# A two-block network in fp32: weight splits of 1024 columns on ScalarE and VectorE in three buffers, in place of 512 columns with GpSimd in six

## The chip, the cores and the metric

One Trainium2 chip, one core. The metric is the device time of one execution in microseconds; lower is better. The kernel before was run three times: median 714.41 us, 713.59 to 714.75.

## What is computed

Two transformer-like blocks, in fp32, on 256 tokens of width 1024.

```python
"block 1"
z = rms_norm(x) @ w_in
q, c_kv, q_idx, k_idx, w_idx, g_attn, x_rnn, g_rnn, merge = split_cols(z)
o = sparse_mla_attention(q, rms_norm(c_kv), q_idx, layer_norm(k_idx), w_idx, w_uk, w_uv)  # top 64 keys by an index score
y_attn = (o * silu(g_attn)) @ w_attn_proj
h = rg_lru(causal_depthwise_conv(x_rnn), ...)             # gates, then a scan over the tokens
y_rnn = (h * silu(g_rnn)) @ w_rnn_proj
x = x + (sigmoid(merge_a) * y_attn + sigmoid(merge_r) * y_rnn) @ w_out
"block 2"
c_q, c_kv, k_r, q_b, k_b, v_b, gate_a, gate_b = jnp.split(rmsnorm(x) @ w_in_2, ...)
o_a = mla_attention(c_q, c_kv, k_r, w_uq, w_ukv)          # low-rank queries, keys, values; rope
o_b = moba_attention(q_b, k_b, v_b)
x = x + (sigmoid(gate_a) * (o_a @ w_o_mla) + sigmoid(gate_b) * (o_b @ w_o_moba)) @ w_out_2
x = x + hierarchical_moe(rmsnorm(x))                      # 32 experts, two of them per token
```

## The kernel before

All weights lie in one array in DRAM, cut into pieces of 1 MB (128 partitions x 2048 fp32), in the order of use. A ring of slots in SBUF takes them (21 of `bigp`, more once the dense part is over); activations that live long take slots of the same ring. SP issues the loads in the order of the pieces, each as soon as its slot is free.

The **dense part** multiplies with fp32 accuracy from three fp32r products. `split` (L233 to L246) takes 512 columns of a piece: ScalarE rounds them to fp32r (`h`, L244), and the rest `l = w - h` is taken by VectorE or GpSimd in turn (L245, `POOLDIV = 2`). `mm3` (L248) then issues h x h and h x l for each k (L254) and l x h (L257). The results of `split` lie in six buffers of 4 KB a partition (`hlp` four, `hl2` two, one split in three). The activations' own high and low halves are made once (`xh`, `xl`; `split_out`, L362 and L363).

`dense_fm` (L263) makes a feature-major result of 256 columns from a piece in four splits of 12 matmuls each; `dense_tm` (L289) makes a token-major one. `dense_tm_last` is the last product before the experts. The names of the pieces tell the stage, in the order of the program: `A`, `qi`, `xr` (input of the recurrence), `q`, `mr`, `ma` (merge gates), `gr`, `rp`, `ga`, `ap`, `wo` (block 1), `cq`, `uq`, `ukv`, `qb`, `kb`, `vb`, `g2a`, `oa`, `g2b`, `ob`, `w` (block 2), then the experts (`gu`, `dn`).

Between the dense pieces, `tick` emits small work from a list: the picks of the top keys (`pick`, L520; the eighth makes the mask `dm`, L527 to L530), the heads' keys and values from `ukuv` (`head_k`, L532, four of 256 columns; `head_v`, two of 512), the recurrence's convolution (`rnn_conv`, L590), gates (`rnn_gate`, L597) and scans (`rnn_scan`, L616; GpSimd's product L620, VectorE's scan L621), and the attention (`ps_s`, L376, the scores; L383, mask and maximum; L384, exponential; L385 and L387, division; `pt`, L394, transposes; `po`, the values). A gate is: `pg` on TensorE (L603), two `rt` on ScalarE (L606), `la` and `tt` (L608, L609), and three VectorE instructions (L611 to L613). `xc`, `rt`, `tt`, `xr`, `wk`, `g` and others are tiles of one pool of seven, `s2p` (NS2 = 7).

In block 2, `p_uq` (three accumulators of 256 columns by two token halves, `mm`, three buffers for all dense products) is evacuated to `qtm` (L878, ScalarE), `p_ukv` to `ktm` and `vm` (L889, L890); the rope on `qtm` is VectorE's (L825 to L828), and `ptm` (L910) transposes them.

The order on each engine is made by the framework's scheduler from the order of the program, estimated durations and priorities. A split, and most evacuations, are emitted `with tc.high_priority(offset=AHEAD)`, AHEAD = 150, which lets them pass what was emitted shortly before. Each engine then runs its own list in order and waits by semaphores.

The **experts** need 64 pieces `gu` and 32 pieces `dn`, multiplied in plain fp32 (L1233, L1260).

Of the kernel before, what the change touches and what calls it, by code (L numbers as in the profile page):

```python
# [17 lines left out]
P = 128  # L18
T = 256
# [5 lines left out]
FILL = -2e38  # L25
NBIG, NMO, NS2, SPARE, POOLDIV = 21, 4, 7, 0, 2
KW = 5
# [52 lines left out]
def tile_two_blocks(ctx: ExitStack, tc: tile.TileContext, w, xT_d, xtk_d, vecs_d, rows_d, consa_d, consb_d, wr_d, lam_d, out_d):  # L80
    nc = tc.nc
# [5 lines left out]
    hl_stack, right_stack = ExitStack(), ExitStack()  # L87
    hlp = [hl_stack.enter_context(tc.tile_pool(name="hlp", bufs=4)), right_stack.enter_context(tc.tile_pool(name="hl2", bufs=2, side="right"))]
    dn = right_stack.enter_context(tc.tile_pool(name="dn", bufs=1, side="right"))
# [142 lines left out]

    def split(view, nk, width, eng=None, small=False):  # L233

        n = nk * width
        if small:
            h, l = (s2(x, F32R)[:, :n].rearrange("p (k c) -> p k c", k=nk) for x in ("h", "l"))
        else:
            hl = (hlp[1] if len(hlp) > 1 and nsplit[0] % 3 == 0 else hlp[0]).tile([P, 1024], F32R, tag="hl", name="hl")
            h, l = (hl[:, o:o + n].rearrange("p (k c) -> p k c", k=nk) for o in (0, 512))  # L240
        nsplit[0] += 1
        e = eng or (nc.gpsimd if nsplit[0] % POOLDIV == 0 else nc.vector)
        with tc.high_priority(offset=AHEAD):
            nc.scalar.activation(h, view, AF.Copy)  # L244
            e.tensor_tensor(l, view, h.bitcast(F32), ALU.subtract)  # L245
        return h, l  # L246
# [16 lines left out]
    def dense_fm(ps, name, rh, rl, nk=8, width=T, c0=0, late=False):  # L263


        wv = piece(name)[:, :nk * width].rearrange("p (k c) -> p k c", k=nk)

        def part(j, q):
            c = c0 + j * P
            h, l = split(wv[:, 4 * q:4 * q + 4, c:c + P], 4, P)  # L270
            return ps[:, j * T:(j + 1) * T], (lambda k: h[:, k - 4 * q, :]), (lambda k: l[:, k - 4 * q, :]), rh, rl
        if late:

            for j in range(2):
                mm3(*part(j, 0), range(4), j == 0, False)
            tick()
            parts = [part(j, 1) for j in range(2)]
            for ks in ((4, 5), (6, 7)):
                for j in range(2):
                    mm3(*parts[j], ks, False, j == 1 and ks[0] == 6)  # L280
        else:
            nq = nk // 4
            for j in range(2):
                for q in range(nq):
                    mm3(*part(j, q), range(4 * q, 4 * q + 4), q == 0, q == nq - 1)
                if j == 0:
                    tick()

    def dense_tm(pss, name, ah, al, nk=8, width=T):  # L289

        wv = piece(name)[:, :nk * width].rearrange("p (k c) -> p k c", k=nk)
        n = min(512 // width, nk)
        one = pss[0] is pss[1]
        for q in range(0, nk, n):
            h, l = split(wv[:, q:q + n, :], n, width)
            for b in range(2):

                mm3(pss[b][:, (b * T if one else 0):][:, :width],
                    lambda k: ah[:, k, b * P:(b + 1) * P], lambda k: al[:, k, b * P:(b + 1) * P],
                    lambda k: h[:, k - q, :], lambda k: l[:, k - q, :], range(q, q + n),  # L300
                    q == 0 and (b == 0 or not one), q + n == nk and (b == 1 or not one))
            if q + n == nk // 2:
                tick()

    def dense_tm_last(pss, name, ah, al, split_done, done):
# [226 lines left out]
    def head_k(i):  # L532
# [999 lines left out]
```

## Time and profile before

| | |
|---|---|
| median of 3 runs | 714.41 us (713.59 to 714.75) |
| the profiled execution | 713.6 us |
| its span, first to last instruction | 711.6 us |
| mean granted clock of TensorE | 0.983 |
| VectorE busy | 416.7 us, 59% of the span, 1035 instructions |
| ScalarE busy | 324.7 us, 46%, 714 instructions |
| GpSimd busy | 238.6 us, 34%, 194 instructions |

The busy time of an engine is a sum over the span, so it hides stages with other limits; the tables by stretches show them. Starts are in microseconds from the span's first instruction. A line such as `L245 DVE TENSOR_TENSOR hl<-w_xr,hl` is one of `split` for the piece `xr`; PE is TensorE, DVE is VectorE, ACT is ScalarE, POOL is GpSimd. Where several instructions are merged into one row (x3), the time runs from the first one's start to the last one's end; consecutive instructions of an engine overlap a little in the records, so the step from one start to the next is what each takes of its engine's time.

### The profile page before, as it was taken

How to read it: one execution, taken by the hardware profiler on the slowest of the kernel's cores; microseconds unless marked ns; L12 is line 12 of the kernel's file. 1: busy time of each engine (PE TensorE's matmuls, PEld its weight loads, DVE VectorE, ACT ScalarE, POOL GpSimd, SP SyncE). 2: the span in 40 equal slices, each digit the busy share in tenths (PEclk: the TensorE clock that was granted, in tenths of full speed). 3: DMA queues.
4: the chain of work that ended last, by engine and by line, in shares of the span. 5: the costliest groups of instructions: out<-in, count | busy, mean ns of one | idle time of the engine just before them, and what ended most of it. 6: DMA issues, size and time to landing. Idle time of an engine off the chain costs nothing. (4 is left out here: it accounts for less than half of the span.)

```text
span 711.6 us, 13956 instructions
## 1 busy us (share of the span) xinstructions
PE 674.1 (95%) x5463; PEld 558.7 (79%) x5463; DVE 416.7 (59%) x1035; ACT 324.7 (46%) x714; POOL 238.6 (34%) x194
## 2 busy tenths in 40 slices
PE   7989999999999999999999999999999999989973
PEld 7989889789999999998999988999645445534532
DVE  4877998789555777889655574375532222222224
ACT  5455598765765656666466466555100000001022
POOL 1454344645535647864332322382000000000002
PEclk8999999999999999999999999999999999999997
DMA  8995116234557457451036615578899999999992
GB/s 314 416 421 212 55 30 252 84 125 172 181 195 275 157 167 292 174 177 66 5 132 221 227 70 195 221 302 319 326 414 421 419 420 420 420 420 420 420 408 76
DMA packets 26855, 178.69 MB, mean 251 GB/s; under 512 B 3104, under 2 KB 4000, under 8 KB 6176
## 3 DMA queue, kind: packets, MB, share of 16 engines
q1 hardware_dynamic: 26352, 177.15, 63.9%
q8 instruction: 45, 0.74, 0.4%
q10 hardware_dynamic: 432, 0.59, 0.2%
q14 instruction: 26, 0.21, 0.1%
HBM read 176.67 MB, written 1.05 MB: 250 GB/s over the span
## 5 line engine op out<-in xcount | busy, mean ns | idle before, releaser
L1316 POOL TENSOR_TENSOR xg<-xo,fin 128x256 f32<-128x256 f32 (+1 forms) x10 | 6.0, 632 | 206.6 <-DVE xo L1306 206.6
L1233 PE MATMUL pgu<-w_gu,xe 128*32 128x512 f32 x512 | 64.9, 597 | 0.4 <-DMA w_gu<-in_w_dram 0.4
L1238 ACT ACTIVATE th<-pgu,ss 128x256 f32<-128x256 f32 x8 | 3.8, 474 | 132.3 <-PE pgu L1233 132.3
L1263 DVE COPY ys<-py 128x256 f32<-128x256 f32 (+1 forms) x33 | 13.7, 416 | 41.8 <-PE py L1260 41.8
L1233 PEld LDWEIGHTS pgu<-w_gu,xe 128*32 128x32 f32 x512 | 14.8, 109 | 28.3 <-issue 25.2
L1197 PEld LDWEIGHTS px<-G,xT 128*128 128x128 f32 x256 | 30.2, 192 | 7.6 <-issue 5.5
L1199 DVE TENSOR_TENSOR xe<-px,vecs 128x256 f32<-128x256 f32 (+1 forms) x34 | 13.8, 409 | 37.3 <-PE px L1197 37.3
L384 ACT ACTIVATE lg<-lg,mx 128x128 f32<-128x128 f32 x64 | 28.3, 444 | 12.1 <-DVE mx L383 12.0
L1197 PE MATMUL px<-G,xT 128*128 128x128 f32 x256 | 31.9, 278 | 1.4 <-DVE G L1185 0.9
L254 PE MATMUL p_qkv<-hl,hh 128*128 128x256 f32 x192 | 33.0, 293 | 0.0
L1339 PE MATMUL acc<-ys,gwT 128*128 128x256 f32 x112 | 29.8, 398 | 2.9 <-DVE ys L1263 2.9
L1339 PEld LDWEIGHTS acc<-ys,gwT 128*128 128x128 f32 x112 | 19.5, 189 | 13.5 <-DVE ys L1263 6.0
L254 PEld LDWEIGHTS p_qkv<-hl,hh 128*128 128x128 f32 x192 | 27.5, 196 | 0.3 <-issue 0.2
L1239 DVE SCALAR_TENSOR_TENSOR th<-th,pgu 128x256 f32<-128x256 f32 x8 | 3.4, 422 | 37.1 <-ACT th L1238 37.1
L387 DVE TENSOR_SCALAR lg<-lg,sm 128x128 f32<-128x128 f32 x64 | 22.2, 391 | 0.8
L257 PE MATMUL p_qkv<-hl,hl__3328 128*128 128x256 f32 x96 | 20.0, 289 | 0.0
L595 DVE SCALAR_TENSOR_TENSOR xc<-xr,vecs,xc 128x256 f32<-128x256 f32 x24 | 18.1, 754 | 1.1 <-ACT xc L593 0.9
L245 POOL TENSOR_TENSOR hl<-w_g2a,hl 128x512 fp32r<-128x512 f32 x8 | 10.4, 1303 | 22.0 <-ACT hl L244 22.0
L254 PE MATMUL p_gr<-xh,hl 128*128 128x256 f32 x64 | 17.3, 299 | 0.0
L254 PE MATMUL p_gr<-xl,hl 128*128 128x256 f32 x64 | 17.3, 297 | 0.0
L245 POOL TENSOR_TENSOR hl<-w_rp,hl 128x512 fp32r<-128x512 f32 x8 | 11.9, 1496 | 15.5 <-ACT hl L244 15.5
L254 PE MATMUL p_cq<-hl__3328,hl 128*128 128x256 f32 x64 | 16.3, 285 | 0.6 <-DVE hl__3328 L755 0.6
(549 smaller groups left out, 2295.1 us busy)
## 6 DMA issues: line engine op xcount, KB each, us to landing
w_gu<-in_w_dram SPq DMA_DIRECT2D x64, 1024.0 KB, 18.2
w_dn<-in_w_dram SPq DMA_DIRECT2D x31, 1024.0 KB, 19.9
w_xr<-in_w_dram SPq DMA_DIRECT2D x4, 1024.0 KB, 11.3
w_q<-in_w_dram SPq DMA_DIRECT2D x4, 1024.0 KB, 17.2
w_mr<-in_w_dram SPq DMA_DIRECT2D x4, 1024.0 KB, 19.8
w_ma<-in_w_dram SPq DMA_DIRECT2D x4, 1024.0 KB, 12.4
w_gr<-in_w_dram SPq DMA_DIRECT2D x4, 1024.0 KB, 5.1
w_rp<-in_w_dram SPq DMA_DIRECT2D x4, 1024.0 KB, 4.9
```

The lines of the kernel that those rows point to most:

```text
L245: e.tensor_tensor(l, view, h.bitcast(F32), ALU.subtract)
L254: nc.tensor.matmul(out, l_(k), r_(k), start=first and i == 0, stop=last and i == n - 1)
L257: nc.tensor.matmul(out, al(k), bh(k), start=first and i == 0, stop=last and i == n - 1)
L384: nc.scalar.activation(lg[:, c0:c1], lg[:, c0:c1], AF.Exp, bias=mx[:, b:b + 1], scale=-1.0, accum_out=sm[:, b:b + 1])
L387: nc.vector.tensor_scalar(lg[:, c0:c1], lg[:, c0:c1], sm[:, b:b + 1], None, ALU.mult)
L595: nc.vector.scalar_tensor_tensor(xc[:, :T], xr[:, kk:kk + T], vec(V_CW, kk * 8 + m), xc[:, :T], ALU.mult, ALU.add)
L1197: nc.tensor.matmul(px[:, j * P:(j + 1) * P], x2[:, k, b, :], G[:, b], start=b == 0, stop=b == 1)
L1199: nc.vector.tensor_tensor(xg[k // 4][:, k % 4:k % 4 + n, :], v3(px, n, P), gain2(k, n), ALU.mult)
L1233: nc.tensor.matmul(pgu[32 * j:32 * j + 32, :], xg[k // 4][:, k % 4, 32 * j:32 * j + 32], wgu[:, 512 * j:512 * j + 512], start=k == 0, stop ...
L1263: nc.vector.tensor_copy(ys[:, :n], py[:, :n])
L1316: nc.gpsimd.tensor_tensor(xg[:, b, sl], xo[:, b, sl], fin[:, sl], ALU.mult)
L1339: nc.tensor.matmul(acc[0][:, b, c // 512, c % 512:c % 512 + n], lhsT, rhs, start=q == 0 and c % 512 == 0, stop=q == 6 and c % 512 == T)
```

## The change

Every split is done by ScalarE (`h`) and VectorE (`l`). A split takes 1024 columns in place of 512; there are three buffers of 8 KB in place of six of 4 KB. Pieces of 2048 columns have two splits; `dense_fm` emits both before its products, `dense_tm` takes 1024 columns at a time with its products in pairs of k (a piece of `uq`, 1536 columns, has a split of 1024 and one of 512, each with a buffer). `head_k`, `head_v`, `A` and the last split of `dense_tm_last` put their halves into two tiles of `s2p` and no longer count for the turn of the buffers. Priorities stay as they were.

```diff
-NBIG, NMO, NS2, SPARE, POOLDIV = 21, 4, 7, 0, 2
+NBIG, NMO, NS2, SPARE = 21, 4, 7, 0
...
-    hlp = [hl_stack.enter_context(tc.tile_pool(name="hlp", bufs=4)), right_stack.enter_context(tc.tile_pool(name="hl2", bufs=2, side="right"))]
+    hlp = [hl_stack.enter_context(tc.tile_pool(name="hlp", bufs=2)), right_stack.enter_context(tc.tile_pool(name="hl2", bufs=1, side="right"))]
...
-    def split(view, nk, width, eng=None, small=False):
+    def split(view, nk, width, small=False):
         n = nk * width
         if small:
             h, l = (s2(x, F32R)[:, :n].rearrange("p (k c) -> p k c", k=nk) for x in ("h", "l"))
         else:
-            hl = (hlp[1] if len(hlp) > 1 and nsplit[0] % 3 == 0 else hlp[0]).tile([P, 1024], F32R, tag="hl", name="hl")
-            h, l = (hl[:, o:o + n].rearrange("p (k c) -> p k c", k=nk) for o in (0, 512))
-        nsplit[0] += 1
-        e = eng or (nc.gpsimd if nsplit[0] % POOLDIV == 0 else nc.vector)
+            hl = (hlp[1] if len(hlp) > 1 and nsplit[0] % 3 == 0 else hlp[0]).tile([P, 2048], F32R, tag="hl", name="hl")
+            h, l = (hl[:, o:o + n].rearrange("p (k c) -> p k c", k=nk) for o in (0, 1024))
+            nsplit[0] += 1
         with tc.high_priority(offset=AHEAD):
             nc.scalar.activation(h, view, AF.Copy)
-            e.tensor_tensor(l, view, h.bitcast(F32), ALU.subtract)
+            nc.vector.tensor_tensor(l, view, h.bitcast(F32), ALU.subtract)
         return h, l
...
         wv = piece(name)[:, :nk * width].rearrange("p (k c) -> p k c", k=nk)
-
-        def part(j, q):
-            c = c0 + j * P
-            h, l = split(wv[:, 4 * q:4 * q + 4, c:c + P], 4, P)
-            return ps[:, j * T:(j + 1) * T], (lambda k: h[:, k - 4 * q, :]), (lambda k: l[:, k - 4 * q, :]), rh, rl
+        if nk == 8:
+            both = [split(wv[:, :, c0 + j * P:c0 + (j + 1) * P], 8, P) for j in range(2)]
+        else:
+            h2, l2 = split(wv[:, :, c0:c0 + 2 * P], nk, 2 * P)
+            both = [(h2[:, :, j * P:(j + 1) * P], l2[:, :, j * P:(j + 1) * P]) for j in range(2)]
+
+        def part(j, ks, first, last):
+            h, l = both[j]
+            mm3(ps[:, j * T:(j + 1) * T], lambda k: h[:, k, :], lambda k: l[:, k, :], rh, rl, ks, first, last)
...
-            nq = nk // 4
             for j in range(2):
-                for q in range(nq):
-                    mm3(*part(j, q), range(4 * q, 4 * q + 4), q == 0, q == nq - 1)
+                for k in range(0, nk, 4):
+                    part(j, range(k, k + 4), k == 0, k + 4 == nk)
                 if j == 0:
                     tick()
 
     def dense_tm(pss, name, ah, al, nk=8, width=T):
...
-        n = min(512 // width, nk)
         one = pss[0] is pss[1]
+        n = 1024 // width
         for q in range(0, nk, n):
-            h, l = split(wv[:, q:q + n, :], n, width)
-            for b in range(2):
...
+            m = min(n, nk - q)
+            h, l = split(wv[:, q:q + m, :], m, width)
+            for q2 in range(q, q + m, 2):
+                for b in range(2):
...
-            if q + n == nk // 2:
+            if q == 0:
                 tick()
 
     def dense_tm_last(pss, name, ah, al, split_done, done):
...
-        for q in (0, 2, 4, 6):
-            hls[q] = split(wv[:, q:q + 2, :], 2, T, nc.vector, small=q == 6)
+        h4, l4 = split(wv[:, 0:4, :], 4, T)
+        hls[0], hls[2] = ((h4[:, q:q + 2, :], l4[:, q:q + 2, :]) for q in (0, 2))
+        hls[4] = split(wv[:, 4:6, :], 2, T)
+        hls[6] = split(wv[:, 6:8, :], 2, T, small=True)
...
-        h, l = split(wA[:, 2 * q:2 * q + 2, :], 2, 200, nc.vector)
+        h, l = split(wA[:, 2 * q:2 * q + 2, :], 2, 200, small=True)
...
-        h, l = split(uu[:, i * T:(i + 1) * T].unsqueeze(1), 1, T)
+        h, l = split(uu[:, i * T:(i + 1) * T].unsqueeze(1), 1, T, small=True)
...
-        h, l = split(uu[:, 1024 + 512 * i:1536 + 512 * i].unsqueeze(1), 1, 512)
+        h, l = split(uu[:, 1024 + 512 * i:1536 + 512 * i].unsqueeze(1), 1, 512, small=True)
...
-        hl2 = [split(wv[:, k:k + 1, 512 * i:512 * i + 512], 1, 512) for k in range(2)]
+        h, l = split(wv[:, :, 512 * i:512 * i + 512], 2, 512)
...
```

The scheduler's lists change with it. Three places follow; names without numbers are tiles, and what an instruction waits for stands in brackets, by engine or DMA queue.

TensorE among the merge gates `p_mr`, where the heads' keys (`p_uk`) and the recurrence's gates (`pg`) are interleaved; before:

```order
476 L254 MATMUL p_mr<-xh,hl 128x256
477 L254 MATMUL p_mr<-xl,hl 128x256
478 L603 MATMUL pg<-xc,w_rg 64x256 [waits DVE_49,PE_49]
479 L603 MATMUL pg<-xc,w_rg 64x256 x3
480 L254 MATMUL p_mr<-xh,hl 128x256 [waits Activation_49]
```

and now:

```order
564 L253 MATMUL p_uk<-cT,h 128x256 [waits PE_49,Activation_49]
565 L253 MATMUL p_uk<-cT,h 128x256
566 L608 MATMUL pg<-xc,w_rg 64x256 [waits DVE_49]
567 L608 MATMUL pg<-xc,w_rg 64x256 x3
568 L256 MATMUL p_uk<-cT,l 128x256 [waits DVE_49]
569 L253 MATMUL p_uk<-cT,h 128x256 x2
570 L256 MATMUL p_uk<-cT,l 128x256
571 L253 MATMUL p_uk<-cT,h 128x256 [waits PE_49,Activation_49]
572 L253 MATMUL p_uk<-cT,h 128x256
573 L608 MATMUL pg<-xc,w_rg 64x256 [waits DVE_49]
574 L608 MATMUL pg<-xc,w_rg 64x256 x3
575 L256 MATMUL p_uk<-cT,l 128x256 [waits DVE_49]
```

Gates 2 to 5 and three `p_uk` stand in a row, with no `p_mr` between them.

ScalarE from the last splits of `uq` on, where `qtm<-p_uq` is the evacuation that frees an accumulator of `p_uq`; before:

```order
380 L244 ACTIVATE hl<-w_ukv 128x512 [waits DMAHW6_49,PE_49,Pool_49]
381 L244 ACTIVATE hl<-w_ukv 128x512 [waits PE_49,Activation_49]
382 L878 ACTIVATE qtm<-p_uq,sqk 128x256 [waits DVE_49]
383 L878 ACTIVATE qtm<-p_uq,sqk 128x256
384 L878 ACTIVATE qtm<-p_uq,sqk 128x256 [waits PE_49]
385 L878 ACTIVATE qtm<-p_uq,sqk 128x256
386 L244 ACTIVATE hl<-w_ukv 128x512 [waits Pool_49]
387 L244 ACTIVATE hl<-w_ukv 128x512 [waits PE_49,Activation_49]
388 L244 ACTIVATE hl<-w_qb_3331 128x512 [waits DMAHW7_49,PE_49,Pool_49]
389 L878 ACTIVATE qtm<-p_uq,sqk 128x256 [waits PE_49]
390 L878 ACTIVATE qtm<-p_uq,sqk 128x256
391 L244 ACTIVATE hl<-w_qb_3331 128x512 [waits Activation_49]
```

and now:

```order
298 L243 ACTIVATE hl<-w_uq_3010 128x1024 [waits DMAHW5_49,PE_49,Activation_49]
299 L243 ACTIVATE hl<-w_uq_3010 128x512 [waits PE_49,Activation_49]
300 L243 ACTIVATE hl<-w_ukv 128x1024 [waits DMAHW6_49,DVE_49,PE_49]
301 L243 ACTIVATE hl<-w_ukv 128x1024 [waits DVE_49,PE_49]
302 L243 ACTIVATE hl<-w_qb_3137 128x1024 [waits DMAHW7_49,DVE_49,PE_49]
303 L883 ACTIVATE qtm<-p_uq,sqk 128x256 [waits DVE_49]
304 L883 ACTIVATE qtm<-p_uq,sqk 128x256 x5
305 L894 ACTIVATE ktm<-p_ukv,sqk 128x4x64 [waits DVE_49,PE_49]
306 L895 ACTIVATE vm<-p_ukv,sqk 128x256
```

All evacuations of `p_uq` moved behind the splits of `ukv` and the first of `qb`.

VectorE at the start of the first attention (`ix<-la,yy` is the scan; `sm` and `lg<-lg,sm` the division; `lg,mx<-ps_s,dm` mask and maximum); before:

```order
217 L621 SCALAR_TENSOR_TENSOR ix<-la,yy 128x256 [waits Pool_49] x3
218 L245 TENSOR_TENSOR hl<-w_gr_855,hl 128x512 [waits Activation_49]
219 L385 RECIPROCAL sm<-sm 128x2 [waits Activation_49]
220 L383 ISA lg,mx<-ps_s,dm 128x128 [waits DVE_49,PE_49]
221 L383 ISA mx 128x1
222 L383 ISA lg,mx<-ps_s,dm 128x256
223 L383 ISA mx 128x1
224 L621 SCALAR_TENSOR_TENSOR ix<-la,yy 128x256 [waits Pool_49]
225 L387 TENSOR_SCALAR lg<-lg,sm 128x128 [waits DVE_49]
226 L387 TENSOR_SCALAR lg<-lg,sm 128x256
```

and now:

```order
226 L390 RECIPROCAL sm<-sm 128x2 [waits Activation_49]
227 L392 TENSOR_SCALAR lg<-lg,sm 128x128 [waits DVE_49]
228 L392 TENSOR_SCALAR lg<-lg,sm 128x256
229 L392 TENSOR_SCALAR lg<-lg,sm 128x128 [waits DVE_49]
230 L392 TENSOR_SCALAR lg<-lg,sm 128x256
231 L388 ISA lg,mx<-ps_s,dm 128x128 [waits DVE_49,PE_49]
232 L388 ISA mx 128x1
233 L686 TENSOR_TENSOR g<-p_ma,s_bc 128x512
234 L388 ISA lg,mx<-ps_s,dm 128x256
235 L388 ISA mx 128x1
236 L626 SCALAR_TENSOR_TENSOR ix<-la,yy 128x256 [waits Pool_49]
```

The divisions of the first heads stand ahead of all scans.

## Rows read from the trace of the kernel before

**Rows 1.** The page's busy time of each engine, share of the span, instructions.
```profile
PE 674.1 (95%) x5463; PEld 558.7 (79%) x5463; DVE 416.7 (59%) x1035; ACT 324.7 (46%) x714; POOL 238.6 (34%) x194
```

**Rows 2.** Stretches: us, busy (x instructions) by engine, PEclk, DMA share, GB/s.
```profile
240.00:260.00 20.00, 20.00 (x170) 20.00 (x170) 14.07 (x19) 12.01 (x21) 12.14 (x9) 1.00 0.49 171
540.00:560.00 20.00, 20.00 (x167) 10.70 (x163) 5.12 (x17) 0.47 (x1) 0.00 (x0) 1.00 1.01 421
```

**Rows 3.** TensorE's waits to 509 us: for whom, us in total, times, longest.
```profile
PE ptm L910 <- DVE qtm L828: 2.5, 1, 2.5
PE ps_s L376 <- DVE mx L383: 1.6, 1, 1.6
PE pt L394 <- DVE lg L387: 1.4, 2, 1.2
PE p_cq L254 <- DVE hl__3328 L755: 0.6, 2, 0.5
```

**Rows 4.** The same table of stretches, right behind two of these waits.
```profile
145.40:148.80 3.40, 3.40 (x17) 3.34 (x16) 3.40 (x8) 2.07 (x5) 1.09 (x1) 0.51 0.20 29
339.90:343.30 3.40, 3.40 (x19) 3.36 (x17) 2.37 (x4) 0.00 (x0) 0.00 (x0) 0.50 0.00 0
```

**Rows 5.** Instructions in time, VectorE and GpSimd, 335 to 339: start, us, what.
```profile
335.58 1.52 DVE L827 TENSOR_TENSOR qtm<-qtm,consb 128x256 f32<-128x256 f32 x1
337.62 1.49 DVE L827 TENSOR_TENSOR qtm<-qtm,consb 128x256 f32<-128x256 f32 x1
...
335.48 1.34 POOL L245 TENSOR_TENSOR hl<-w_qb,hl 128x512 fp32r<-128x512 f32 x1
337.56 1.27 POOL L245 TENSOR_TENSOR hl<-w_qb,hl 128x512 fp32r<-128x512 f32 x1 [0.74 <-ACT hl L244]
```

**Rows 6.** The same, 132 to 144, VectorE and GpSimd.
```profile
132.79 3.37 DVE L621 TENSOR_TENSOR_SCAN ix<-la,yy 128x256 f32<-128x256 f32 x3 [1.59 <-POOL yy L620]
139.83 3.30 DVE L621 TENSOR_TENSOR_SCAN ix<-la,yy 128x256 f32<-128x256 f32 x2
...
132.02 7.66 POOL L620 TENSOR_TENSOR yy<-yy,ix 128x256 f32<-128x256 f32 x8 [4.62 <-ACT yy L619]
139.64 4.56 POOL L245 TENSOR_TENSOR hl<-w_gr,hl 128x512 fp32r<-128x512 f32 x3
```

**Rows 7.** L245 to 509 us; groups (busy us, mean ns); one convolution step.
```profile
0.00:509.00 509.00, 122.01 (x144) 189.84 (x135) 0.99 0.53 199
...
L245 DVE TENSOR_TENSOR hl<-w_g2b,hl 128x512 fp32r<-128x512 f32 x8 | 5.5, 693 | 8.4 <-ACT hl L244 8.4
L363 DVE TENSOR_TENSOR oa<-po,oa 128x256 fp32r<-128x256 f32 x4 | 1.7, 425 | 3.1 <-ACT oa L362 3.1
L452 ACT ACTIVATE xtk<-xtk 128x1024 f32<-128x1024 f32 x2 | 2.1, 1048 | 1.4 <-DMA xtk<-in_xtk_dram 1.4
...
96.96 0.48 DVE L595 SCALAR_TENSOR_TENSOR xc<-xr,vecs,xc 128x256 f32<-128x256 f32 x1
```

**Rows 8.** ScalarE in time around one gate.
```profile
98.66 0.83 ACT L606 ACTIVATE rt<-pg,hb 128x256 f32<-128x256 f32 x2
99.37 0.60 ACT L608 ACTIVATE la<-rt,nsp 128x256 f32<-128x256 f32 x1
100.35 0.63 ACT L244 ACTIVATE hl<-w_mr 128x512 fp32r<-128x512 f32 x1
```

**Rows 9.** ScalarE's evacuations of p_uq, and first p_ukv on TensorE.
```profile
326.50 1.57 ACT L878 ACTIVATE qtm<-p_uq,sqk 128x256 f32<-128x256 f32 x4 [0.25 <-DVE sqk L862]
...
331.28 1.09 PE L254 MATMUL p_ukv<-hl,cqp 128*128 128x512 f32 x4
```

**Rows 10.** 80 to 120 us: all engines as in rows 2; then L595 alone.
```profile
80.00:120.00 40.00, 39.98 (x311) 35.29 (x310) 38.02 (x75) 33.35 (x71) 17.67 (x14) 1.00 0.37 131
...
80.00:120.00 40.00, 13.17 (x18) 1.00 0.37 131
```

More of the change, by code (lines that the diff above doesn't have):

```diff
@@ L266, in dense_fm @@
         wv = piece(name)[:, :nk * width].rearrange("p (k c) -> p k c", k=nk)
-        def part(j, q):
-            c = c0 + j * P
-            h, l = split(wv[:, 4 * q:4 * q + 4, c:c + P], 4, P)
-            return ps[:, j * T:(j + 1) * T], (lambda k: h[:, k - 4 * q, :]), (lambda k: l[:, k - 4 * q, :]), rh, rl
+        if nk == 8:
[6 more added lines that the diff above has]
+            mm3(ps[:, j * T:(j + 1) * T], lambda k: h[:, k, :], lambda k: l[:, k, :], rh, rl, ks, first, last)
         if late:
             for j in range(2):
-                mm3(*part(j, 0), range(4), j == 0, False)
+                part(j, range(4), j == 0, False)
             tick()
-            parts = [part(j, 1) for j in range(2)]
             for ks in ((4, 5), (6, 7)):
                 for j in range(2):
-                    mm3(*parts[j], ks, False, j == 1 and ks[0] == 6)
+                    part(j, ks, False, j == 1 and ks[0] == 6)
         else:
-            nq = nk // 4
             for j in range(2):
-                for q in range(nq):
-                    mm3(*part(j, q), range(4 * q, 4 * q + 4), q == 0, q == nq - 1)
+                for k in range(0, nk, 4):
+                    part(j, range(k, k + 4), k == 0, k + 4 == nk)
                 if j == 0:
@@ L291, in dense_tm @@
         wv = piece(name)[:, :nk * width].rearrange("p (k c) -> p k c", k=nk)
-        n = min(512 // width, nk)
         one = pss[0] is pss[1]
+        n = 1024 // width
         for q in range(0, nk, n):
-            h, l = split(wv[:, q:q + n, :], n, width)
-            for b in range(2):
[L298 to L301, printed above, removed]
-            if q + n == nk // 2:
+            m = min(n, nk - q)
+            h, l = split(wv[:, q:q + m, :], m, width)
+            for q2 in range(q, q + m, 2):
+                for b in range(2):
+                    mm3(pss[b][:, (b * T if one else 0):][:, :width],
+                        lambda k: ah[:, k, b * P:(b + 1) * P], lambda k: al[:, k, b * P:(b + 1) * P],
+                        lambda k: h[:, k - q, :], lambda k: l[:, k - q, :], range(q2, q2 + 2),
+                        q2 == 0 and (b == 0 or not one), q2 + 2 == nk and (b == 1 or not one))
+            if q == 0:
                 tick()
@@ L885, in tile_two_blocks @@
             mm3(ps, lambda k: cqp[:, 6 + k, b * P:(b + 1) * P], lambda k: cql[:, 6 + k, b * P:(b + 1) * P],
-                lambda k: hl2[k][0][:, 0, :], lambda k: hl2[k][1][:, 0, :], range(2))
+                lambda k: h[:, k, :], lambda k: l[:, k, :], range(2))
             p4 = ps.rearrange("p (h c) -> p h c", h=4)
```

## The prediction

> **What bounds the kernel now.** I read the busy shares first: TensorE works 674.1 of 711.6 us [rows 1]. The table by stretches [rows 2] says with which limit. From 240 to 260 us TensorE is busy 20.00 of 20 us with 170 matmuls, one every 118 ns, at a granted clock of 1.00; VectorE, ScalarE and GpSimd have more than a quarter of that time free. From 540 on the DMA share is 1.01 at 421 GB/s: the experts' weights set the pace. The two parts are joined by slots. Weights that TensorE has not used yet fill all slots by the end of the dense part, and a new transfer starts when TensorE empties one. A microsecond won or lost before about 510 us therefore moves the end by one; "costs" and "gains" below mean that.
>
> So only TensorE's own waits before 510 us can be won. The list of waits [rows 3] has 2.5 us for `ptm` (VectorE, `qtm`), 1.6 for `ps_s`, 1.4 for `pt`, 0.6 for `p_cq`. Two of these places cost more than they wait: behind each, the granted clock is 0.50 or 0.51 for 3.4 us [rows 4], the lower of its two levels (1.2 for 2.4 GHz), which is 1.7 us of work lost each time.
>
> What held VectorE in both places? Before `ptm` [rows 5]: two rope multiplications (L827) took 1.52 and 1.49 us, and each lies over a GpSimd weight split (1.34 and 1.27 us). Another VectorE instruction with two operands of that size needs 0.425 (L363 in [rows 7]). Before `ps_s` and `pt` [rows 6]: two scans (L621) of 3.30 us together stand on VectorE in front of the mask addition that frees `ps_s`; GpSimd's products for the scans, and then three splits, run beside them. The lengthening is general: L245 on VectorE takes 122.01 us for 144 instructions, 0.85 each, where those of `w_g2b` take 0.69 [rows 7].
>
> **What the change does.** *GpSimd's splits go to VectorE, two in one.* 135 instructions and 189.84 us leave GpSimd [rows 7]. A split of 512 columns costs VectorE 0.69 and one of 256 columns 0.425, so I estimate 0.69 + 2 x 0.265 = 1.23 us for 1024 columns, 0.61 a half. 135 x 0.61 = 82 us come to VectorE; its own 144 get 0.08 shorter each (-11), and the lengthening that goes is 144 x 0.16 = 23 us on the splits and as much again or more on convolutions, ropes and gates. VectorE's total hardly moves, and where TensorE has no gap it is not on the path: there this edit costs nothing, and its cover is VectorE's free time (5.9 of 20 us from 240 to 260 [rows 2]). ScalarE's half of a split, 0.63 us at 512 columns [rows 8], becomes 1.05 at 1024 by the nearest instruction of that size (L452 [rows 7]); two of 0.63 become one, so ScalarE gains time. TensorE's products are the same in number; their order within a piece, and the small tiles for `w_A`, change nothing on the path.
>
> *Three buffers for six.* A split waits for the buffer of the split three before it. Two buffers ahead are 48 matmuls, 48 x 0.118 = 5.7 us (before, five of 12: 7.1 us). A split takes 1.05 + 1.23 = 2.3 us, so it is hidden while ScalarE and VectorE are less than about 3.4 us behind with other work. If they are more, TensorE waits for the difference.
>
> The Trainium skill, "Perfetto Trace Analysis", section "Optimizing Scalar/DVE Operations", speaks against wider splits: where these engines are not saturated but cause bubbles elsewhere, breaking instructions up may finish work sooner. By that rule a wait for a split grows by 0.42 us on ScalarE and 0.54 on VectorE. From 240 to 260 us there is no bubble to grow [rows 2]; the sum by the rule would differ only in new wait 2 below, by 0.4.
>
> *The stalls that go.* At `ptm` no split runs on GpSimd any more, and TensorE now has 24 `p_qkv` matmuls (2.8 us) in front of `ptm`: -2.5, and -1.7 for the clock, -4.2. At the start of the attention VectorE's order now has the first heads' divisions (L387, now L392) ahead of all scans, where they stood behind four: the 1.4 and 1.6 us of `pt` and `ps_s` [rows 3] go with their clock drop, -4.7. What would be late next is the split behind the first scan; I find no more than half a microsecond and count none. `p_cq`, -0.6: the instruction that it waits for has GpSimd's split beside it. These gains are bounded by nothing at one end and all of it, -9.5, at the other.
>
> *New wait 1, the recurrent gates.* `head_k` and `head_v` now take two tiles each of the small pool of seven, which the convolution and gate tiles share. So the gates of steps 2 to 5 come in a bunch, as TensorE's order shows: `p_uk` and `pg` in turn, and no `p_mr` between them. Each `p_uk` waits for ScalarE's split, which stands behind the gate's own work. By ScalarE's back-to-back starts [rows 8] that is two `rt` 0.71, two `kTs` of the same shape 0.71, `la` and `tt` 0.98, and the split about 0.4 (256 columns): 2.8 us, with semaphores 3.0. TensorE has four `p_uk` (0.48) meanwhile and waits 2.5. In the next step `kTs` stands behind the split: 2.3 - 0.5 = 1.8. Then some 0.4 for a low half and for `p_mr`, whose accumulator VectorE empties late. Together 4.7 us; before, the gates lay between dense runs and cost nothing. I add one clock drop, 1.7, since both stretches with waits of this size had one [rows 4]. Bounds: nothing, if VectorE's relief lets the early gates go sooner; 4.7 + 3 x 1.23 + 2 x 1.7 = 11.8, if a wide split stands in front of each step on VectorE too.
>
> *New wait 2, `p_ukv`.* ScalarE's queue now has the first split of `w_qb` ahead of the evacuations of `p_uq` (`qtm`). Its buffer is that of the last `w_uq` split, which TensorE gives back only when `p_uq` is done; and `p_ukv` needs the first `p_uq` accumulator. The wait: 1.05, two evacuations at 1.57 / 4 = 0.39 [rows 9], and 0.15 of semaphores, 2.0 us. Before, four evacuations were done at 328.1, and `p_ukv` began at 331.28, as soon as `p_uq` ended. Bounds 0 and 2.0 + 1.7. I take 2.0 without a clock drop: the wait is shorter than the two with one, and full runs of `p_uq` and `p_ukv` lie around it.
>
> The sum: -4.2 - 4.7 - 0.6 + 4.7 + 1.7 + 2.0 = **-1.1 us**. It is made against the profiled execution, 713.6 us (of which 2.0 lie outside the span); that is 0.8 below the median of 714.41, from which I forecast 713.3.
>
> **The rivals.** *A, the gates cost nothing.* VectorE, freed of the lengthening (18 convolution steps took 13.17 us from 80 to 120 [rows 10]; at the 0.48 of an undisturbed one [rows 7] they take 8.6), gives the small tiles back so early that the bunch dissolves. Then -9.5 + 2.0 = -7.5: 706.9, and 704.9 without wait 2. For it: the lengthening is large just there. Against it: the order is fixed in the program, and the 2.8 us are ScalarE's.
>
> *B, slower: the scans keep the attention's stall.* GpSimd's eight products for the scans stay, 7.66 us, and the first scans were long (3.37 us for three) before a split ran on GpSimd [rows 6]. If VectorE reaches the first divisions only behind scans, or late behind a wide split, `pt` waits as before: +4.7, sum +3.6, 718.0. It decides whether the first `pt` still comes after a scan. Against it: the order.
>
> *C, slower: the small pool starves.* New wait 1 at its upper bound and a clock drop at wait 2: 11.8 + 3.7 - 9.5 = +6.0, 720.4, if it is VectorE that ends each step.
>
> *D, VectorE becomes the bound.* From 80 to 120 us it works 38.02 of 40 [rows 10], with 14 splits on GpSimd beside it. Those bring 14 x 0.61 = 8.5. If none of the lengthening went, 46.5 us of work would cost +6.5 in place of the 4.7 of wait 1, so +0.7 in all, 715.1. The rows speak against it: the 4.6 us on the convolutions alone take it back to 42, and splits and gates have more. The same section of the skill's page would have a saturated VectorE give work to others, even GpSimd, not take it; it adds that these two share a port, so that it might not help. With that second half the trace agrees: 1.52 us for 0.425 [rows 5].
>
> **How the numbers follow.** The forecast 0.38, A 0.24, B 0.14, C 0.12, D 0.12. The forecast's own range is 711.5 to 715, one clock drop more or less. The whole range, 706 to 719.5, leaves out the lower half of A and most of C. A measurement of this kernel can tell 0.2%, 1.4 us. Faster than 713.0: A and 0.17 of the forecast, 0.41. Slower than 715.8: B, C, and 0.03 of the others, 0.29. The rest, 0.30.
>
> **What would show it.** Right: `ptm` and `pt` leave the list of TensorE's waits; `p_uk` waits for ScalarE with about 4 us and `p_ukv` with about 2; one stretch of half clock lies near the gates, none near 145 and 340; L245's mean at 1024 columns is 1.2 us with no long ones. Wrong: `pt` or `ps_s` still wait (B); `p_uk` waits for nothing (A); it waits much longer, and for VectorE (C); many short waits for VectorE's half between 80 and 120 (D). Dense matmuls that wait for a split between 160 and 290 would say that three buffers are too few, which I hold for covered.

## The result, and the profile after

The change made the kernel slower: 718.9 us as the median of six runs (714.33 to 720.49) against 714.3 (712.86 to 714.75), a ratio of 1.0057, 95% interval 1.004 to 1.0074. Forecast was 713.3. The profiled execution took 720.49 us, the longest of the six, with a span of 718.7; it is 1.6 us above its median, the one before 0.7 below its own, so the profiles differ by more (7.1 us in span) than the medians (4.6).

The page's busy times [rows 1], now:

```profile
PE 678.5 (94%) x5463; PEld 560.9 (78%) x5463; DVE 428.1 (60%) x1038; ACT 305.7 (43%) x582; POOL 52.1 (7%) x59
```

GpSimd is nearly out of it, and VectorE has only 11.4 us more in all: it took on the splits and lost the lengthening. The splits' low halves alone, to 509 us [rows 7]; then 80 to 120 us [rows 10] (columns: us; busy and count of PE, PEld, DVE, ACT, POOL, or of VectorE alone; PEclk, DMA share, GB/s):

```profile
0.00:509.00 509.00, 173.59 (x147) 0.98 0.52 193
...
80.00:120.00 40.00, 35.58 (x276) 31.45 (x275) 32.31 (x75) 26.10 (x48) 0.00 (x0) 0.97 0.29 106
```

The 147 splits take 173.59 us where 144 took 122.01 with another 135 on GpSimd; a convolution step is 0.48 us everywhere. From 80 to 120 us VectorE is busy 32.31 us, not 38.02. So VectorE is no bound (rival D). TensorE's waits to 509 us [rows 3]:

```profile
PE p_uk L253 <- ACT h L243: 4.4, 2, 2.8
PE pA L253 <- ACT h L243: 2.1, 1, 2.1
PE p_ukv L253 <- ACT qtm L883: 1.9, 1, 1.9
PE p_w L253 <- DVE hl L244: 1.1, 1, 1.1
...
PE pt L399 <- DVE lg L392: 1.0, 1, 1.0
PE ptA L490 <- DVE misc L481: 0.9, 1, 0.9
PE ps_i L513 <- ACT rl L517: 0.6, 1, 0.6
PE ps_i L513 <- DVE misc L493: 0.5, 1, 0.5
PE p_cq L253 <- DVE hl__3134 L760: 0.4, 1, 0.4
PE po L408 <- ACT pT L401: 0.3, 1, 0.3
```

`ptm` and `ps_s` have left the list, `p_uk` and `p_ukv` have come, as forecast. `pt`, which was to leave it too, still waits 1.0. `ptA` (the transposes of the index keys, at 36 us) was not in the forecast. The granted clock by stretches [rows 4] shows its weight:

```profile
39.00:45.60 6.60, 6.60 (x30) 5.95 (x31) 6.42 (x12) 4.17 (x7) 0.10 (x1) 0.50 1.01 421
117.60:120.90 3.30, 3.30 (x16) 2.62 (x13) 2.12 (x6) 3.28 (x9) 0.00 (x0) 0.50 0.00 0
145.40:148.80 3.40, 3.40 (x22) 2.47 (x21) 2.92 (x12) 3.37 (x9) 0.00 (x0) 1.00 0.01 2
339.70:342.70 3.00, 3.00 (x8) 2.35 (x8) 2.63 (x13) 1.15 (x3) 1.68 (x2) 0.50 0.84 336
```

The drop at 145 is gone; the one at 340 is there still, now behind `p_ukv`; one stands behind the gates; and a new one, twice as long, lies at 39 to 45.6 us, right behind the index scores (`ptA`, `ps_i`). Before, that stretch ran at 1.00, although `ps_i` waited 0.7 and 0.6 us then too:

```profile
39.00:45.60 6.60, 6.60 (x56) 6.27 (x55) 6.60 (x9) 5.79 (x12) 5.42 (x5) 1.00 1.02 426
```

Where the 7.1 us of the spans went is seen by following the n-th of TensorE's dense products (all of L254, L257 and L317, now L253, L256 and L320). Starts in us, two experiments below beside them; "experts" is the first product of that stage (`px`):

```
dense product   144   216   1080   2016   2304   3168  experts   end
before         30.1  42.8  179.5  304.3  352.7  484.8    509.2  711.6
after          29.5  46.0  185.6  309.7  357.4  490.6    515.3  718.7
b512_dve       28.7  44.7  178.6  301.9  346.0  478.9    503.3  706.7
b512_dve_xr    29.4  41.6  177.0  300.3  344.4  477.3    501.7  704.2
```

Differences of the first two lines, stretch by stretch: index stage (144 to 216) +3.8; gates and first attention (216 to 1080) +2.9; then -0.7; `uq` to `ukv` (2016 to 2304) -0.7; to the end of block 2 +1.1 and +0.3; the experts +1.0.

**The index stage.** VectorE and TensorE in time, 34 to 39 us (start, us, what, idle time before):

```profile
35.45 0.69 DVE L649 TENSOR_TENSOR xr<-p_xr,s_bc 128x512 f32<-128x512 f32 x1 [0.63 <-PE p_xr L256]
36.06 0.29 DVE L481 COPY misc<-misc 128x64 f32<-128x64 f32 x2
...
36.30 0.44 PE L490 MATMUL ptA<-consa,misc 128*128 128x128 f32 x2 [0.89 <-DVE misc L481]
```

The evacuation of the first `p_xr`, which has priority, now stands on VectorE ahead of the key copies (L481) that `ptA` needs. It waits for TensorE, the copies behind it wait too, and TensorE then waits for the copies. Before, the copies (then L476) ran ahead of the evacuation, and `ptA` had no wait:

```profile
34.38 0.32 DVE L476 COPY misc<-misc 128x64 f32<-128x64 f32 x2
36.06 0.69 DVE L644 TENSOR_TENSOR xr<-p_xr,s_bc 128x512 f32<-128x512 f32 x1 [1.36 <-PE p_xr L257]
```

**The gates.** TensorE and ScalarE:

```profile
111.95 0.50 PE L253 MATMUL p_uk<-cT,h 128*128 128x256 f32 x2 [2.83 <-ACT h L243]
...
109.04 0.84 ACT L611 ACTIVATE rt<-pg,hb 128x256 f32<-128x256 f32 x2 [1.80 <-PE p_uk L253]
109.77 0.84 ACT L548 ACTIVATE kTs<-p_uk,vecs 128x256 f32<-128x256 f32 x2
110.49 0.61 ACT L613 ACTIVATE la<-rt,nsp 128x256 f32<-128x256 f32 x1
110.98 0.61 ACT L614 ACTIVATE tt<-rt,sp 128x256 f32<-128x256 f32 x1
111.47 0.42 ACT L243 ACTIVATE h<-w_ukuv 128x256 fp32r<-128x256 f32 x1
```

This is the chain of new wait 1: `rt`, `kTs`, `la`, `tt`, then the split, 2.8 us.

Two things more belong to the stretch from 216 to 1080. Rows 3 shows four waits of a longer list; two more of that list lay here before and are gone:

```profile
PE pg L603 <- ACT rt L606: 0.6, 1, 0.6
PE p_xr L257 <- DVE hl L245: 0.6, 1, 0.6
```

And the 40 `ps_s` products take TensorE 1.5 us more, which no list of waits shows (columns: us; busy and count of TensorE; PEclk, DMA share, GB/s), before and after:

```profile
42.80:179.50 136.70, 6.08 (x40) 0.99 0.41 154
46.00:185.60 139.60, 7.63 (x40) 0.99 0.37 140
```

Before, most of them stood as eight of two heads side by side; now other products stand between many of the heads' fours. The last section has what that does.

**`p_ukv`.** VectorE, ScalarE, TensorE:

```profile
336.93 0.23 DVE L867 TENSOR_TENSOR sqk<-rs_y,s 128x2 f32<-128x2 f32 x2
...
336.76 1.06 ACT L243 ACTIVATE hl<-w_qb 128x1024 fp32r<-128x1024 f32 x1 [0.37 <-DVE hl L244]
337.72 2.28 ACT L883 ACTIVATE qtm<-p_uq,sqk 128x256 f32<-128x256 f32 x6
...
338.59 1.48 PE L253 MATMUL p_ukv<-hl,cqp 128*128 128x512 f32 x4 [1.88 <-ACT qtm L883]
```

`qtm` stands behind the split of `w_qb`, as forecast. But `sqk`, the scale that `qtm` needs, came only at 336.93 too: between the small steps that make it, from 328.55 on, VectorE's order has eight scalings of `xT` (L951) that the broadcast for block 2 (`block2_bcast`) releases. Two causes end within 0.7 us of each other: `sqk` is done at 337.2, the split at 337.8, and `qtm` follows the split.

### The profile page after: what moved, and what is told of

It reads as the page before. It is cut to its first block, busy times and chain, and to the rows that moved or that the text cites. A ratio compares the mean times of both kernels' runs of the same rounds, so it can differ in the third digit from the quotient of the medians.

```text
span 718.7 us, 13515 instructions
## 1 busy us (share of the span) xinstructions
PE 678.5 (94%) x5463; PEld 560.9 (78%) x5463; DVE 428.1 (60%) x1038; ACT 305.7 (43%) x582; POOL 52.1 (7%) x59
## 5 line engine op out<-in xcount | busy, mean ns | idle before, releaser
L253 PE MATMUL p_qkv<-hl,hh 128*128 128x256 f32 x192 | 31.9, 286 | 0.0
L253 PEld LDWEIGHTS p_qkv<-hl,hh 128*128 128x128 f32 x192 | 26.5, 190 | 0.3 <-issue 0.2
L256 PE MATMUL p_qkv<-hl,hl__3134 128*128 128x256 f32 x96 | 19.8, 284 | 0.0
L392 DVE TENSOR_SCALAR lg<-lg,sm 128x128 f32<-128x128 f32 x64 | 18.3, 331 | 0.7
L253 PE MATMUL p_w<-hl,m2h 128*128 128x256 f32 x96 | 16.4, 287 | 1.1 <-DVE hl L244 1.1
L253 PE MATMUL p_xr<-xh,hl 128*128 128x256 f32 x64 | 17.5, 301 | 0.0
L253 PE MATMUL p_xr<-xl,hl 128*128 128x256 f32 x64 | 17.3, 299 | 0.0
L253 PE MATMUL p_mr<-xh,hl 128*128 128x256 f32 x64 | 16.9, 293 | 0.0
L253 PE MATMUL p_rp<-hgh,hl 128*128 128x256 f32 x64 | 16.7, 293 | 0.0
L253 PE MATMUL p_mr<-xl,hl 128*128 128x256 f32 x64 | 16.7, 290 | 0.0
```

Of the source, the lines that this page charges most:

```text
L253: nc.tensor.matmul(out, l_(k), r_(k), start=first and i == 0, stop=last and i == n - 1)
L256: nc.tensor.matmul(out, al(k), bh(k), start=first and i == 0, stop=last and i == n - 1)
L392: nc.vector.tensor_scalar(lg[:, c0:c1], lg[:, c0:c1], sm[:, b:b + 1], None, ALU.mult)
```

## The experiments

Theories at the start: the loss comes from the heads' splits in the small pool (small-pool theory), or from VectorE's added load, or from splits that are twice as wide with half the buffers. All nine kernels were compared with the kernel before, run beside them.

**b512_dve**: the kernel before, with every low half on VectorE.

```diff
-        e = eng or (nc.gpsimd if nsplit[0] % POOLDIV == 0 else nc.vector)
+        e = nc.vector
```

> The kernel before, with GpSimd's weight splits given to VectorE and nothing else (512 columns, six buffers, no small tiles). If the loss of the change comes from VectorE's added work (theory V), this is slower than before as the change is, by 3 us or more. If it comes from the order and the buffers (theory S: the small pool, and three wide buffers), GpSimd's absence is a gain here: the rope ahead of ptm takes 0.42 us each, the 2.5 us wait for ptm and the clock drop behind it go, 709 to 713 us.

Measured: 710.07 us (708.51 to 711.91, 6 runs) against 714.24; ratio 0.9945 [0.993, 0.996]. TensorE's waits to 520 us, and the same split totals:

```profile
...
PE ptA L485 <- DVE misc L476: 2.4, 1, 2.4
PE po L403 <- ACT pT L396: 2.1, 1, 2.1
...
0.00:509.00 509.00, 196.50 (x279) 0.99 0.54 201
```

Taking GpSimd off the splits is a gain by itself, 4.2 us, though VectorE's own splits rise from 122 to 196.5 us. `ptm`, `ps_s` and `pt` are gone; at the attention's start `po` waits 2.1 us in their place. VectorE's load is not what made the change slow. `ptA` waits here too, longer than after the change, with a stretch of half clock from 37 to 43.6 us behind it.

**a1024_pool**: the change, with the low half of every second wide split on GpSimd.

```diff
-            nc.vector.tensor_tensor(l, view, h.bitcast(F32), ALU.subtract)
+            (nc.gpsimd if not small and nsplit[0] % 2 == 0 else nc.vector).tensor_tensor(l, view, h.bitcast(F32), ALU.subtract)
```

> The change, with every second wide split's low half back on GpSimd. Theory V: back to 714. Theory S: the p_uk waits of some 4 us may move but the time stays at 716 or above, since the wide buffers and the small tiles stay; GpSimd's half of 1024 columns takes about 2.6 us and lengthens VectorE's two-operand instructions again, so 718 to 723 is possible.

Measured: 742.75 us (739.47 to 745.12, 5 runs); ratio 1.0387 [1.0368, 1.0406], far above the 718 to 723 expected. Two of its split groups (shortest, median and longest in ns, then the first and last start):

```profile
L244 POOL TENSOR_TENSOR hl<-w_mr,hl x4: 2367/2392/2443, 85.5 to 110.2; 128x1024 fp32r<-128x1024 f32 x4
L244 DVE TENSOR_TENSOR hl<-w_mr,hl x4: 1218/1226/2827, 86.2 to 106.7; 128x1024 fp32r<-128x1024 f32 x4
```

A wide split takes GpSimd 2.4 us. Most of VectorE's beside it keep their 1.22, single ones take up to 2.8. That is no longer hidden: six of TensorE's tiles wait 2.5 us or more in all (`p_cq` 4.9, for VectorE's splits of `w_cq`, two of which take 2.57 and 2.73). So wide splits don't go with GpSimd taking every second one; another sharing wasn't run.

**a_heads_hl**: the change, with `head_k` and `head_v` back in the large buffers.

```diff
-        h, l = split(uu[:, i * T:(i + 1) * T].unsqueeze(1), 1, T, small=True)
+        h, l = split(uu[:, i * T:(i + 1) * T].unsqueeze(1), 1, T)
...
-        h, l = split(uu[:, 1024 + 512 * i:1536 + 512 * i].unsqueeze(1), 1, 512, small=True)
+        h, l = split(uu[:, 1024 + 512 * i:1536 + 512 * i].unsqueeze(1), 1, 512)
```

> The change, with the splits of head_k and head_v in the three wide buffers again, so that the small pool is free of them. Theory S: the gates spread out between dense runs, the p_uk waits (2.8 and 1.6 us) and the clock drop at 118 us go, 6 us faster than the change: 711 to 714. Theory V: the waits for the low half stay, no more than 1 us faster.

Measured: 711.56 us (708.35 to 716.72, 12 runs); ratio 0.9972 [0.995, 0.9995]; 7.3 below the change. `p_uk` waits for nothing; in its place `ps_s` 2.3 and `pg` 1.8 remain. From dense product 216 to 1080 it takes 135.4 us, the change 139.6: the pool is worth 4.2 us of its profile. The waits make little of that, 4.1 us in place of 4.4; half clock behind `p_uk` (1.7) and the parted `ps_s` products (6.02 us here, 7.63 in the change) make more. Its execution also had no half-clock stretch in the index stage (14.0 us against 16.5) and none behind `p_ukv`, though the waits there are the same as after the change.

**a_bcast_late**: the change, with the broadcast for block 2 two pieces of `uq` later (not one, as the expectation has it).

```diff
         if i == 0:
             latent_scales()
+        if i == 2:
             block2_bcast()
```

> The change, with the broadcast and scaling of the token scales (eight VectorE instructions on xT) emitted one uq piece later, so that the scale of qtm is done early and the evacuations of p_uq stand ahead of the first split of qb. If the p_ukv wait (1.9 us) is the order of VectorE's scale chain and ScalarE's list, it goes, and with it the clock drop at 340 us: 2 to 4 us faster than the change, 715 to 717. If it is the buffer alone, the wait stays above 1 us.

Measured: 716.48 us (713.12 to 720.95, 12 runs); ratio 1.0032 [1.0011, 1.0052]; 2.4 below the change, with intervals that overlap. The wait at `p_ukv` and the drop at 340 us are gone. But the two causes went together: `sqk` is done at 330.2, and on ScalarE the first `qtm` now stand ahead of a split of `w_ukv`, and so ahead of `w_qb`:

```profile
330.13 1.57 ACT L884 ACTIVATE qtm<-p_uq,sqk 128x256 f32<-128x256 f32 x4 [1.45 <-DVE sqk L867]
331.57 1.07 ACT L243 ACTIVATE hl<-w_ukv 128x1024 fp32r<-128x1024 f32 x1
```

Whether one of the two would have been enough is not shown. How much the gain is worth, the next runs show.

**b512_small**: `b512_dve`, with the heads' splits in the small pool (the diff of `a_heads_hl` the other way round).

> The kernel before with every low half on VectorE, and the halves of head_k and head_v in tiles of the small pool; splits stay 512 columns wide in six buffers. With the change itself, a_heads_hl and b512_dve this completes a square: width and buffers one way, heads in the small pool the other. Small-pool theory: TensorE's order again has p_uk and pg of gates 2 to 5 in a row, and p_uk waits for ScalarE's h with 3 to 5 us in all, with one stretch of half clock near it; the time is 5 to 8 us above b512_dve, about 716. Rival, wide splits: the bunch costs only where a split of 1024 columns stands in ScalarE's and VectorE's queues ahead of the gate's own work; then p_uk waits under 1 us and the time is that of b512_dve, 710 within 1.

Measured: 715.43 us (713.67 to 716.76, 12 runs); ratio 1.0019 [1.001, 1.0028]. Its waits, and the stretch behind them:

```profile
PE p_uk L254 <- ACT h L244: 3.9, 2, 2.8
...
113.00:121.00 8.00, 6.94 (x32) 4.62 (x33) 5.18 (x12) 5.85 (x15) 0.00 (x0) 0.57 0.00 0
```

With splits of 512 columns in six buffers the small pool costs 5.4 us, at the same place, by the same chain: the small-pool theory holds, its rival (wide splits in the queue) falls. A part is again the parted `ps_s` products, 7.63 us in place of 6.02 in `b512_dve`. The square now reads: GpSimd off -4.2; heads in the small pool +5.4; width and buffers +3.5 (715.4 to 718.9; the small tiles of `w_A` come with it). By its other corner, `a_heads_hl`: width and buffers +1.5 (710.1 to 711.6, not clear of the noise), then the small pool +7.3.

**a_gates_kv**: `a_heads_hl` and `a_bcast_late` together.

> The change with both repairs: head_k and head_v split into hl buffers again, and the broadcast for block 2 emitted two pieces of uq later. If the two losses are separate places, their gains add: a_heads_hl's 711.6 less the 2.4 us that a_bcast_late took off, 709.2 (0.993 of before). p_uk and p_ukv wait for nothing; what remains is ptA 0.9, ps_i 1.1 in the index stage, p_w 1.1 and about 0.7 at pt. Rival: the time only follows how many stretches of half clock an execution happens to have; then it stays at 711 to 712 with the same spread of 8 us.

Measured: 716.14 us (711.12 to 717.57, 12 runs); ratio 1.001 [0.9988, 1.0031]. A miss: the two gains don't add; it is slower than `a_heads_hl`, and its rival's 711 to 712 didn't come either. `p_ukv` waits for nothing; but TensorE's work on the tile `po` from 300 to 500 us (PE and PEld busy, then DVE, ACT) is longer, first `a_heads_hl`:

```profile
300.00:500.00 200.00, 7.87 (x64) 4.48 (x64) 3.37 (x8) 3.05 (x8) 1.00 0.50 183
```

and `a_gates_kv`:

```profile
300.00:500.00 200.00, 10.43 (x64) 5.74 (x64) 3.36 (x8) 3.06 (x8) 1.00 0.48 176
```

No wait is listed there. In the new order other products stand between the `po` products of two heads. TensorE in time, `a_heads_hl`:

```profile
380.42 0.66 PE L408 MATMUL po<-pT,vm 128*64 128x256 f32 x4
380.91 0.39 PE L409 MATMUL po<-pT,vm 128*64 128x128 f32 x4
381.23 0.50 PE L253 MATMUL p_qkv<-hl,hh 128*128 128x256 f32 x2
```

and `a_gates_kv`:

```profile
384.36 0.65 PE L408 MATMUL po<-pT,vm 128*64 128x256 f32 x2
384.85 0.38 PE L409 MATMUL po<-pT,vm 128*64 128x128 f32 x2
385.16 0.62 PE L253 MATMUL p_qkv<-hl,hh 128*128 128x256 f32 x3
```

Side by side, the eight of both heads take 0.81 us to the next product; parted, the four of one head take 0.80. In sum that costs 2.56 us, more than the 1.9 saved. (`a_bcast_late` has the same 10.43 us, the change itself 7.87.)

**a_three**: `a_gates_kv`, with the first evacuation of `p_xr` taken off VectorE.

```diff
+            if i:
                 nc.vector.tensor_tensor(xr[:, :, 3:259], v3(ps), bc2(s_bc, 2), ALU.mult)
+            else:
+                nc.scalar.activation(xr[:, :, 3:259], v3(ps), AF.Copy)
+                nc.gpsimd.tensor_tensor(xr[:, :, 3:259], xr[:, :, 3:259], bc2(s_bc, 2), ALU.mult)
```

> As a_gates_kv, and the first evacuation of p_xr taken off VectorE (ScalarE copies, GpSimd multiplies), so that the key copies which ptA waits for are no longer behind it. Theory of the index stage: the wait of ptA (0.9 us) goes and with it some of the stretches of half clock at 39 us; 0.9 to 4 us below a_gates_kv, 706 to 708. Rival: the ps_i waits (0.5 and 0.6) behind ptA stay and keep the clock drop, so only 0.9 goes, or nothing, because the work that follows is late for another reason.

Measured: 713.35 us (711.66 to 714.71, 12 runs); ratio 0.9988 [0.998, 0.9997]. It is 2.8 below `a_gates_kv`, so the step from there is as expected; the absolute 706 to 708 is missed with the base. `ptA` waits no more, and the clock is 1.00 from 36 to 45 us although `ps_i` still waits 0.5 and 0.6.

**a_heads_xr**: `a_three` without the late broadcast.

> a_heads_hl (the change with head_k and head_v split into hl buffers, broadcast of block 2 where it was) with the first evacuation of p_xr taken off VectorE as in a_three. In its order the two heads' po products stand side by side again. If the late broadcast cost what it gave by parting them, this kernel keeps p_ukv's wait of 1.9 us and po at 7.9 us in all, against 10.4 in a_three, so it is 0 to 1 us below a_three, and below a_heads_hl by the ptA wait (0.9) and a part of the half-clock stretches near 39 us: 709 to 712. If width costs nothing but the waits p_ukv and p_w that remain (1.9 and 0.8), it lies 3 us above b512_dve_xr, 709.5. Rival: the late broadcast was a gain that the clock hid; then it is slower than a_three, 714 or more.

Measured: 710.56 us (707.81 to 713.07, 6 runs); ratio 0.9942 [0.9922, 0.9961]. `po` is back at 7.88 us, `p_ukv` waits 1.9 again, and still it is the faster one, by 2.8 us, more than expected: with the heads' splits in the large buffers the late broadcast is in sum a loss. `po` explains 0.7 of that (2.56 less 1.9). Both profiles with both repairs also have a half-clock stretch among the experts, near 630 us, which may be chance (below); this one has its stretch behind `p_ukv` instead. The rest is open. Against `b512_dve_xr` (below) it is 4.0 us slower, where 3 was worked out from `p_ukv` and `p_w`.

**b512_dve_xr**: `b512_dve` with the same edit for `p_xr`.

> b512_dve (512 columns, six buffers, every low half on VectorE) with the first evacuation of p_xr taken off VectorE in the same way. There ptA waited 2.4 us behind it and a stretch of half clock from 37 to 43.6 us followed. Index-stage theory: that wait goes, and with it the stretch: 2.4 + 3.3 = 5.7 us below b512_dve's profiled execution, so 705 to 708 as a median, the fastest of all. Rival: the wait goes, the clock falls all the same behind ps_i's waits: 707.5 to 708.5.

Measured: 706.57 us (705.8 to 707.57, 4 runs) against 714.19; ratio 0.9901 [0.9886, 0.9915]. This is the fastest, faster than both kernels. Of the waits in the index stage `ps_i` remains (0.6 and 0.5); the stretch:

```profile
36.00:45.00 9.00, 8.13 (x65) 7.40 (x66) 7.46 (x17) 6.64 (x14) 1.20 (x2) 1.00 1.01 420
```

The 2.4 us at `ptA` and the half clock behind them are gone; 3.5 us of median come from taking one instruction off VectorE. (The median lies in the 705 to 708 forecast; of the 5.7 between profiled executions 2.5 came, as this one has another drop, at 155 us behind `po`, and a longer one in its first 20 us.)

## Why the prediction was wrong

The sign was wrong: -1.1 us was forecast and +4.6 came (medians), at the upper end of the range. Step by step, by the profiled executions, in which the price of a clock drop is that of one execution:

- **The stalls that go** (-4.2, -4.7, -0.6). `ptm` went whole. Of the attention's start 1.0 (`pt`) and 0.3 (`po`) remain: VectorE runs two scans and then a split of 1.19 us ahead of a division. That is the "split behind the first scan" that I had counted as none; -3.4 in place of -4.7. `p_cq` kept 0.4 of 0.6.
- **New wait 1** (4.7 and 1.7). Right in size and cause: 4.4 at `p_uk`, one half-clock stretch of 3.3 us. Without the bunch in the same kernel (`a_heads_hl`) that wait goes (two others, 4.1 us, come), and with it in the other width (`b512_small`) it comes. Rival A, that the gates cost nothing, falls. Not foreseen: the bunch also parts the `ps_s` products, 1.5 us. And the gates did not "cost nothing" before: `pg` waited 0.6.
- **New wait 2** (2.0). 1.9 came, but by two causes at once, of which I had named one; and a clock drop of 1.7 followed, which I had left out because the wait is short. (No row stood behind the 0.2 and 0.15 for semaphores in the two new waits; their longest came to 2.8 and 1.9 with all in.)
- **"there this edit costs nothing, and its cover is VectorE's free time"** (that of 240 to 260). This is the step that failed. I took the free time of a steady stretch as cover for every place that had no large wait, and so the sum has no term for the index stage. There the cover is the order of VectorE's list, and the edit changed it: `ptA` waits 0.9 us and 3.4 us are lost to half clock behind it, 3.8 in all by dense products 144 to 216. I had looked for what becomes late only at places that I already knew to wait. `b512_dve`, GpSimd's removal alone, has the same wait, longer. With the one evacuation away the wait and the drop go; the medians fall by 2.8 (`a_three` against `a_gates_kv`) and 3.5 us (`b512_dve_xr` against `b512_dve`). These price it better than one profile's drop.
- **Width.** Also missed: `p_w` waits 1.1 us for a split of `w_w` that takes VectorE 2.32 us instead of 1.22, beside two of GpSimd's few instructions:

```profile
479.53 2.32 DVE L244 TENSOR_TENSOR hl<-w_w,hl 128x1024 fp32r<-128x1024 f32 x1
...
479.15 1.62 POOL L1024 TENSOR_TENSOR mt<-mt,tga 128x512 f32<-128x512 f32 x1 [1.82 <-DVE mt L1023]
480.71 1.29 POOL L1041 CAST trir<-consa 128x128 fp32r<-128x128 f32 x1
```

  With 512 columns `p_w` waits 0.3 (`b512_small`). The same kernel but for width and buffers (and `w_A`'s tiles) is slower by 3.5 us (715.4 to 718.9), by 4.0 (`b512_dve_xr` 706.6, `a_heads_xr` 710.6) and by 1.5 (710.1 to 711.6). The Trainium skill's rule that I had weighed, in "Perfetto Trace Analysis", section "Optimizing Scalar/DVE Operations" (broken-up instructions may finish work sooner), agrees with that in sign. How much of it is width and how much the number of buffers, no run separates; `p_ukv` and `p_w` make up 1.9 + 0.8 of it. Long dense runs do hide it, as I had said: TensorE has no gap from 180 to 300 us.
- **The experts** add 1.0 to the span: `pgu` waits 1.6 us for weights, before 0.4. I had counted them as moving with the dense part.

The sum again, measured: index +3.8; gates +6.1, attention -3.4, the waits of `pg` and `p_xr` that went -1.2, `ps_s` +1.5 (together +3.0 for +2.9); `uq` to `ukv` -4.2 + 1.9 + 1.7 = -0.6; `p_w` +1.1; the experts +1.0. With -0.7 in the dense run (`p_cq` and small gaps), +0.3 at its end and -0.6 before product 144 these make 7.3 of terms for the 7.1 of the spans. B and C named times near the result. Of B's mechanism 1.3 of 4.7 us came: `pt` and `po` still wait, `pt` behind scans and a split, but `ps_s` doesn't. C's did not: `p_uk` ended on ScalarE. That their times are near is luck.

## What to carry to other kernels

When work moves to another engine, walk through every place where that engine feeds the bound one and compare the two orders there, also where nothing waits yet; free time in a steady stretch says nothing about a stage that is a chain. A tile moved to a small shared pool binds steps that had nothing to do with each other. And of a change in several parts, run the parts: here GpSimd's removal alone was worth 4.2 us, and 7.6 with one evacuation out of the way; the pool and the width turned the 4.2 into a loss of 4.6.

## What I had not expected of the hardware

The clock isn't the same from one execution to the next. `a_heads_hl` took 708.4 us at a mean granted clock of 0.995 and 716.7 at 0.981, and the other ten lie between, in the order of the clock but for one pair. Its waits in the index stage are those of `a_gates_kv`, 0.9, 0.5 and 0.6 us, but the clock behind them differs; 38 to 45 us, first `a_heads_hl`:

```profile
38.00:45.00 7.00, 6.95 (x58) 6.49 (x57) 6.33 (x10) 4.02 (x7) 0.00 (x0) 1.00 1.01 421
```

and `a_gates_kv`:

```profile
38.00:45.00 7.00, 6.43 (x31) 5.48 (x28) 6.15 (x12) 4.75 (x8) 0.10 (x1) 0.55 1.02 422
```

`a_bcast_late` has these three waits too, and its profile has clock 1.00 there. So a drop behind waits of this size comes in some executions and not in others; one profile doesn't give its price. The twelve runs of `a_gates_kv` lie in two groups, four at 711.1 to 711.9 us with a mean clock of 0.989 to 0.993 and eight at 715.5 to 717.6 with 0.981 to 0.985. The four kernels with these three waits spread over 6.2 to 8.4 us; those without the wait at `ptA`, or with 2.4 us and more there, over 1.8 to 5.7. That the short waits make the spread is likely, not shown.

The second is the pairing of `po`: two heads' products of 64 columns, side by side, take the time of one head's (0.81 and 0.80 us), so that a product moved between them costs without any wait in the list. `ps_s`, with 64 rows, does the same: in the kernel before, eight of two heads from 133.48 us take 0.86 us to the next product; in the change, four of one head from 145.83 take 0.85.
